# Alternating the halves of the accumulation bank between pairs of heads in a chunked RWKV-7 recurrence

## The chip, the cores and the metric

The kernel runs on one core of a Trainium2 chip. It is written with explicit instructions for the engines: TensorE (PE, matrix products, which write to PSUM banks of 128 partitions x 512 float32), VectorE (DVE), ScalarE (ACT), GpSimd (POOL) and SyncE, which issues transfers. The metric is the time of one execution on the device, in microseconds, as the median of several runs.

## The reference, cut to what matters

The program is one layer of a decoder trunk for 256 tokens of width 2048, all in float32: a mixer, an MLP and a gated embedding. Half of the mixer is an RWKV-7 recurrence with 16 heads of 64 channels:

```python
def step(S, inp):
    r_t, w_t, k_t, v_t, a_t, b_t = inp
    sa = jnp.einsum('bhij,bhj->bhi', S, a_t)
    S = S * w_t[:, :, None, :] + sa[..., None] * b_t[:, :, None, :] + v_t[..., None] * k_t[:, :, None, :]
    y = jnp.einsum('bhij,bhj->bhi', S, r_t)
    return S, y
...
mu = jnp.mean(y, axis=-1, keepdims=True)
var = jnp.mean(jnp.square(y - mu), axis=-1, keepdims=True)
y = (y - mu) * lax.rsqrt(var + GN_EPS) * gn_g.astype(f32).reshape(H, N) + gn_b.astype(f32).reshape(H, N)
```

Around it stand the other half of the mixer (moving averages over 2, 4, 8 and 16 tokens with a product), the products with `w_in`, `w_out`, the MLP (2048 to 8192 and back) and the gate.

## The kernel before, in words

**Chunks instead of steps.** The recurrence is not run token by token. The 256 tokens are cut into four chunks of 64, and the 16 heads into two groups of eight (`gi` 0 and 1), that is four pairs of heads each. Within a chunk everything is a product of small matrices. For each group, earlier stages make: `AR`, the decayed rows (for each pair and chunk, 64 columns for the state's reading `a` and 64 for the output's reading `r`, in the order i = 0, 1); `SC`, the masked scores of the chunk, whose upper left part has been replaced by the inverse of a triangular matrix; `UV`, with corrections `u` in partitions 0 to 63 and centred values `v` in 64 to 127; `BKt`, the decayed sources for the state's update.

**`rwkv_core(gi, st)`** runs the four chunks one after the other. A chunk `c` has one PSUM bank `b` (`rym`), whose lower 64 partitions collect the right-hand sides and whose upper 64 collect the outputs, 64 columns for each head:

1. `direct` (L695) adds the part of the right-hand sides that doesn't need the state; contraction over partitions 64 to 127. For chunk 0 it stands alone; for the later chunks it is issued one chunk ahead, head by head between the products of step 4. `bank(c)` (L691) first issues a product of one zero column with the start flag into the upper half, so that the outputs there accumulate from a clean state.
2. For c > 0 one product per pair (L707, 128x128) adds the state `cur` read through `AR[:, p, c]`: the 64 `a` columns go to the lower half of the bank, the 64 `r` columns to the upper.
3. ACT copies the lower half to SBUF as `R` (L713, 64x512).
4. The inverse is applied: `ub = SC[0:64, 0] x R` (L727), and ACT copies it to `UV[c][0:64]` (L731).
5. For c < 3 the state's update `sb` (L736) is computed; even heads go to partitions 0 to 63 and odd heads to 64 to 127 of another bank. ACT (c = 0, L745) or DVE (L747, after a decay in L718) puts it into the next state.
6. The outputs: `SC[:, 1] x UV[c]` for each head, added to the upper half of `b` (L749), and ACT copies it to `yss` (L754, 64x512).
7. For chunks 1 and 3, `group_norm` (L777 to L781) and, one chunk later, `group_out` (L787, L789).

A float32 product is two instructions in the trace, so the eight heads of a step are 16.

**What fills the waits.** PE's order is written out by hand (`manual_schedule`): the text of the program is PE's order. Between the steps stands `fill(us)`, which takes products of the queued large matrix products (`zv`, `zp`, `o0a`, `o1a`...; L164 to L166 and L173 to L175) for about the given microseconds by a fixed estimate per product, so their number between two steps is fixed. Each of them needs its weights split in two parts: ACT writes a rounded copy `wh` (L151, two instructions), DVE the remainder `wl` (L152), from three buffers. The order on the other engines comes from a planner with priorities; splits have 20000, the evacuations of `R` and `ub` 30000. `group_norm` has 25000.

**Beside it.** While the first group's core runs, DVE also works on `inverse(1, st1)` for the second group, 31 steps of two instructions (L621, L625), then four transposes (L630, L634), which ACT writes back into `SC` (L638). `rwkv_merge` (L649) uses it. While the second group's core runs there is no such work.

**Tiles.** Work tiles come from one pool by tag; a tag with one buffer is handed on when the last reader of the tile before is done. Tag `tA` holds the decay `P` of the second group until `rwkv_r(1)` has read it (L546), then nothing until the pooling after the first core. Tag `tE` is the work tile `tmp` of `inverse(1)` until ACT has read it out.

Of the kernel before, what the change touches and what calls it, by code (L numbers as in the profile page):

```python
# [9 lines left out]
F32 = mybir.dt.float32  # L10
F32R = mybir.dt.float32r
AF = mybir.ActivationFunctionType
# [28 lines left out]
def trunk(  # L41
# [19 lines left out]
    nc = tc.nc  # L61

    const = ctx.enter_context(tc.tile_pool(name="const", bufs=1))
# [9 lines left out]
    def rw_bank(name):  # L73
        return psr.tile([128, 512], F32, tag="rw", name=name)
# [33 lines left out]
    nc.gpsimd.memset(rmask.rearrange("p (c t) -> p c t", t=64)[:, :, 0:1], 0.0)  # L108
    for i in range(2):
        nc.vector.memset(sbd[i], 0.0)  # L110
    zero64 = const.tile([128, 64], F32, name="zero64")
    nc.vector.memset(zero64, 0.0)
    edge = const.tile([128, 4, 16], F32, name="edge")
    nc.vector.memset(edge, 1.0)
    for g, win in enumerate(WINDOWS):
# [118 lines left out]
    def fill(us):  # L234

        while us > 0 and queue:
            us -= advance()
# [44 lines left out]
    def e4(tag):  # L282
        return rp.tile([128, 4, T], F32, tag=tag, name=f"{tag}_t")
# [55 lines left out]
    for kg, (tg, n) in enumerate((("tE", 1), ("tF", 2), ("zk", 3), ("zr", 3), ("zv", 3), ("BK", 2), ("BKt", 2))):  # L339
# [13 lines left out]
        if kg == 4:  # L353
            for tt in range(2):
                for i, q in enumerate((2, 3)):
                    nc.tensor.matmul(
                        sbank[:, tt : tt + 1], sums[q][:, 0, tt * 128 : (tt + 1) * 128], ones[:, 0:1],
                        start=i == 0 and tt == 0, stop=i == 1, skip_group_check=True,
# [83 lines left out]
    def yb(gi, i):  # L442
        if gi == 0:
            return ybuf[:, i * 1024 : (i + 1) * 1024].rearrange("p (a t) -> p a t", a=4)
        return e4(("tF", "tC")[i])
# [235 lines left out]
    def rwkv_core(gi, st):  # L681
        AR, pc, SC, BKt, UV = st["AR"], st["pc"], st["SC"], st["BKt"], st["UV"]

        YT = yb(gi, 1)
        Rs = rp.tile([64, 2, 8, 64], F32, tag="q2", name=f"R{gi}")
        yss = rp.tile([128, 2, 8, 64], F32, tag="q3", name=f"ys{gi}")

        def bank(c):

            b = rw_bank("rym")  # L690
            nc.tensor.matmul(b[64:128, 0:1], zero64[64:128], zero64[64:128, 0:1], start=True, stop=False, skip_group_check=True)  # L691
            return b

        def direct(b, c, h):
            nc.tensor.matmul(  # L695
                b[0:64, h * 64 : h * 64 + 64], SC[64:128, 0, c, h, :], UV[c][64:128, h, :],
                start=h == 0, stop=c == 0, skip_group_check=True,
            )

        b = bank(0)  # L700
        for h in range(8):
            direct(b, 0, h)
        for c in range(4):
            cur, nxt = sbd[c % 2], sbd[(c + 1) % 2]
            if c > 0:
                for p in range(4):
                    nc.tensor.matmul(  # L707
                        b[:, p * 128 : p * 128 + 128], AR[:, p, c].rearrange("j i t -> j (i t)"), cur[:, p, :],
                        start=False, stop=False, skip_group_check=True,
                    )  # L710
            R = Rs[:, c % 2]
            with tc.high_priority(30000):
                nc.scalar.activation(flat3(R), b[0:64, :], AF.Copy)  # L713
            if 0 < c < 3:
                for e in range(2):
                    r = slice(e * 64, e * 64 + 64)
                    with tc.high_priority(30000):
                        nc.vector.tensor_tensor(  # L718
                            nxt[r, :, r], cur[r, :, r], pc[r, :, c : c + 1].to_broadcast([64, 4, 64]), op=ALU.mult
                        )  # L720
            fill(1.1)
            ub = rw_bank("um")
            if c < 3:
                sb = rw_bank("sm")
                b_next = bank(c + 1)
            for h in range(8):
                nc.tensor.matmul(ub[0:64, h * 64 : h * 64 + 64], SC[0:64, 0, c, h, :], R[:, h, :], start=True, stop=True)  # L727
                if c < 3:
                    direct(b_next, c + 1, h)
            with tc.high_priority(30000):  # L730
                nc.scalar.activation(flat3(UV[c])[0:64], ub[0:64, :], AF.Copy)  # L731
            fill(1.1)
            if c < 3:
                for h in range(8):
                    e, p = h % 2, h // 2
                    nc.tensor.matmul(  # L736
                        sb[e * 64 : e * 64 + 64, p * 64 : p * 64 + 64], BKt[:, c, p, e * 64 : e * 64 + 64], UV[c][:, h, :],
                        start=True, stop=True,
                    )
                add = sb[:, 0:256].rearrange("j (p i) -> j p i", i=64)  # L740
                for e in range(2):
                    r = slice(e * 64, e * 64 + 64)
                    with tc.high_priority(30000):
                        if c == 0:
                            nc.scalar.activation(nxt[r, :, r], add[r], AF.Copy)  # L745
                        else:
                            nc.vector.tensor_tensor(nxt[r, :, r], nxt[r, :, r], add[r], op=ALU.add)  # L747
            for h in range(8):
                nc.tensor.matmul(  # L749
                    b[64:128, h * 64 : h * 64 + 64], SC[:, 1, c, h, :], UV[c][:, h, :],  # L750
                    start=False, stop=True, skip_group_check=True,
                )
            ys = yss[:, c // 2]
            nc.scalar.activation(flat3(ys)[(c % 2) * 64 : (c % 2) * 64 + 64], b[64:128, :], AF.Copy)  # L754
            b = b_next
            if c == 1:
                norm0 = group_norm(gi, 0, yss[:, 0])
            if c == 2:
                group_out(gi, 0, norm0, YT)
            if c < 3:  # L760
                fill(1.6)
        return YT, st["rk"], yss
# [7 lines left out]
    def flat3(t_):  # L770
        return t_.rearrange("s h i -> s (h i)")

    def group_norm(gi, tt, ysb):
        with tc.high_priority(25000):
            vs = rp.tile([128, 8], F32, tag="gv", bufs=2, name=f"gv{gi}{tt}")
            sq = rp.tile([128, 8, 64], F32, tag="sq", name=f"sqy{gi}{tt}")
            nc.scalar.activation(sq, ysb, AF.Square)  # L777
            nc.vector.tensor_reduce(vs, sq, axis=AX.X, op=ALU.add)
            nc.scalar.activation(vs, vs, AF.Sqrt, bias=eps_g, scale=1.0 / 64.0)
            nc.vector.reciprocal(vs, vs)  # L780
            nc.vector.tensor_tensor(ysb, ysb, vs.unsqueeze(2).to_broadcast([128, 8, 64]), op=ALU.mult)  # L781
        return ysb

    def group_out(gi, tt, ysb, YT):
        b = rw_bank("yt")
        for p in range(4):
            nc.tensor.transpose(b[:, p * 128 : (p + 1) * 128], flat3(ysb)[:, p * 128 : (p + 1) * 128], ident)  # L787
        for p in range(4):
            nc.scalar.activation(  # L789
                YT[:, p, tt * 128 : (tt + 1) * 128], b[:, p * 128 : (p + 1) * 128], AF.Identity,  # L790
                scale=col("gn_g", 4 * gi + p), bias=col("gn_b", 4 * gi + p),
            )
# [122 lines left out]
    beside += [inverse(1, st1), 0.95, 0.0]  # L915
    fill(1.5)
    core0 = rwkv_core(0, st0)
    mg0 = a8(0, "mg0", F32R)
    rwkv_out(0, *rwkv_norm1(0, *core0), mg0)
# [30 lines left out]
    ]  # L950
    fill(1.5)
    core1 = rwkv_core(1, st1)
    finish(p_zp1)
    pws1 = pool_weights(1)
# [400 lines left out]
```

## Time and profile before

The median of three runs is 1205.03 us, from 1204.11 to 1207.36. The page shows one profiled execution, with a span of 1198.9 us; no time of its own beside that span is given for it.

| what | value |
|---|---|
| median of runs | 1205.03 us |
| span of the profiled execution | 1198.9 us |
| PE, DVE, ACT, POOL busy in it | 1179.6, 868.1, 687.7, 15.4 us |
| first core (chunks of group 0) | about 194 to 228 us |
| second core (group 1) | about 272 to 306 us |
| L749, one instruction | 0.22 us, x128 |

A row of the order of time has the start in us from the beginning of the span, the duration, the engine, the line, the operation, what is written from what, the shape and the count. Consecutive instructions of one kind are merged: the duration then runs from the first start to the last end. In brackets stands the idle time of the engine before the row and what ended it. Matrix products overlap, so a duration of 0.22 us does not mean that the next starts 0.22 us later; the distance of the starts has to be read.

### The profile page before, as it was taken

Reading aid. Unit: us, or ns where it says so; the run is one execution under the profiler, and the core shown is the slowest. Engines: PE = TensorE matmul, PEld = TensorE weight load, DVE = VectorE, ACT = ScalarE, POOL = GpSimd, SP = SyncE. Lnnn points to the kernel's source line nnn. Section 1 sums busy time; section 2 is a strip of 40 time slices with the busy share of each in tenths; the row PEclk is TensorE's granted clock in tenths of the full one; section 3 lists DMA queues with packets and bytes.
Section 4 is the critical chain, followed back from the end, with each engine's and each line's share of the span. In section 5 each row is a group of like instructions: output and inputs, shape, how many; then the busy total and the mean of one; then the engine's idle time right before and its main releaser. Section 6 shows DMA issues by size and latency. Waiting matters only on the chain.

```text
span 1198.9 us, 18442 instructions
## 1 busy us (share of the span) xinstructions
PE 1179.6 (98%) x7076; PEld 1013.6 (85%) x7076; DVE 868.1 (72%) x1150; ACT 687.7 (57%) x1260; POOL 15.4 (1%) x65
## 2 busy tenths in 40 slices
PE   8999999999999999999999999999999999999996
PEld 6999988988888888888888788888888888778886
DVE  8687987854556667666888878666667888887552
ACT  6857565665545556555555555555555655668544
POOL 4000000000000000000000000000000000000000
PEclk9999999999999999999999999999999999999999
DMA  7463542354355565666665666665565655776631
GB/s 250 151 202 110 173 155 95 121 186 142 116 177 169 185 185 191 192 193 189 194 203 197 197 197 203 195 187 189 192 193 178 211 198 191 290 234 219 194 121 71
DMA packets 60328, 216.88 MB, mean 181 GB/s; under 512 B 6736, under 2 KB 7120, under 8 KB 59856
## 3 DMA queue, kind: packets, MB, share of 16 engines
q1 hardware_dynamic: 59952, 215.19, 55.1%
q8 instruction: 55, 0.90, 0.3%
q10 hardware_dynamic: 288, 0.52, 0.1%
q14 instruction: 33, 0.27, 0.1%
HBM read 213.59 MB, written 2.10 MB: 180 GB/s over the span
## 4 chain that ended last, share of the span: by engine, by line
PE 81%; DMA 6%; DVE 6%; ACT 4%; issue 2%; SPq 0%; ACTq 0%; DVEq 0%
PE u_w L986 20%; PE u_w L990 10%; DMA raw_d<-in_w_ffn_down_dram 5%; PE d_b L1101 4%; PE d_b L1100 4%; PE d_b L1102 4%; PE gt_b L173 2%; PE gt_b L175 2%; PE gt_b L174 2%; PE zv_b L164 1%; PE zp_b L173 1%; PE wag_b L333 1%; PE zv_b L165 1%; PE zv_b L166 1%; PE zp_b L175 1%
## 5 line engine op out<-in xcount | busy, mean ns | idle before, releaser
L986 PE MATMUL u_w<-h,wh_u 128*128 128x512 f32 x1024 | 355.4, 393 | 0.0
L990 PE MATMUL u_w<-h,wl_u 128*128 128x256 f32 x1024 | 285.5, 279 | 0.0
L151 ACT ACTIVATE wh_u<-raw_u 128x512 fp32r<-128x512 f32 x256 | 147.6, 624 | 162.9 <-PE u_w L986 82.0
L152 DVE TENSOR_TENSOR wl_u<-raw_u,wh_u 128x1024 fp32r<-128x1024 f32 x128 | 156.6, 1224 | 112.1 <-ACT wh_u L151 112.1
L986 PEld LDWEIGHTS u_w<-h,wh_u 128*128 128x128 f32 x1024 | 191.8, 187 | 43.2
L990 PEld LDWEIGHTS u_w<-h,wl_u 128*128 128x128 f32 x1024 | 193.1, 189 | 0.1
L152 DVE TENSOR_TENSOR wl_gt<-raw_gt,wh_gt 128x1024 fp32r<-128x1024 f32 x24 | 29.4, 1225 | 23.9 <-ACT wh_gt L151 23.9
L151 ACT ACTIVATE wh_gt<-raw_gt 128x512 fp32r<-128x512 f32 x48 | 27.8, 631 | 23.0 <-PE gt_b L175 20.4
L1140 DVE TENSOR_TENSOR td<-raw_d 128x512 f32<-128x512 f32 x22 | 15.2, 692 | 33.9 <-DMA raw_d<-in_w_ffn_down_dram 33.9
L164 PE MATMUL zv_b<-hTh,wh_zv 128*128 128x256 f32 x128 | 37.7, 294 | 0.0
L173 PE MATMUL gt_b<-wh_gt,h 128*128 128x512 f32 x96 | 37.5, 390 | 0.0
L164 PE MATMUL zr_b<-hTh,wh_zr 128*128 128x256 f32 x128 | 37.5, 293 | 0.0
L175 PE MATMUL gt_b<-wh_gt,h 128*128 128x512 f32 x96 | 37.4, 389 | 0.0
L174 PE MATMUL gt_b<-wl_gt,h 128*128 128x512 f32 x96 | 37.4, 389 | 0.0
L166 PE MATMUL zr_b<-hTh,wl_zr 128*128 128x256 f32 x128 | 37.2, 290 | 0.1
L164 PE MATMUL zk_b<-hTh,wh_zk 128*128 128x256 f32 x128 | 37.0, 289 | 0.0
L165 PE MATMUL zr_b<-hTl,wh_zr 128*128 128x256 f32 x128 | 36.9, 288 | 0.0
L165 PE MATMUL zk_b<-hTl,wh_zk 128*128 128x256 f32 x128 | 36.3, 284 | 0.5 <-DVE hTl L157 0.5
L166 PE MATMUL zk_b<-hTh,wl_zk 128*128 128x256 f32 x128 | 36.3, 284 | 0.2 <-DVE wl_zk L152 0.2
L166 PE MATMUL zv_b<-hTh,wl_zv 128*128 128x256 f32 x128 | 36.2, 283 | 0.0
L165 PE MATMUL zv_b<-hTl,wh_zv 128*128 128x256 f32 x128 | 36.2, 283 | 0.0
L156 ACT ACTIVATE wad<-raw_d 128x512 fp32r<-128x512 f32 x22 | 13.9, 632 | 36.6 <-DMA raw_d<-in_w_ffn_down_dram 34.5
(804 smaller groups left out, 3081.4 us busy)
## 6 DMA issues: line engine op xcount, KB each, us to landing
raw_u<-in_w_ffn_up_dram SPq DMA_DIRECT2D x128, 512.0 KB, 3.5
raw_d<-in_w_ffn_down_dram SPq DMA_DIRECT2D x128, 512.0 KB, 4.2
raw_gt<-in_w_ple_gate_dram SPq DMA_DIRECT2D x24, 512.0 KB, 3.5
raw_zk<-in_w_in_dram SPq DMA_DIRECT2D x16, 512.0 KB, 3.3
raw_zr<-in_w_in_dram SPq DMA_DIRECT2D x16, 512.0 KB, 3.3
raw_zv<-in_w_in_dram SPq DMA_DIRECT2D x16, 512.0 KB, 3.3
raw_zp<-in_w_in_dram SPq DMA_DIRECT2D x16, 512.0 KB, 3.2
raw_o<-in_w_out_dram SPq DMA_DIRECT2D x16, 512.0 KB, 3.5
```

The costliest lines, as they stand in the source:

```text
L151: nc.scalar.activation(wh[:, a * 512 : (a + 1) * 512], raw[:, a * 512 : (a + 1) * 512], AF.Copy)
L152: nc.vector.tensor_tensor(wl, raw, wh.bitcast(F32), op=ALU.subtract)
L164: nc.tensor.matmul(o, w_h, ah, start=first and ct % 2 == 0, stop=False, skip_group_check=True)
L165: nc.tensor.matmul(o, w_h, al, start=False, stop=False, skip_group_check=True)
L166: nc.tensor.matmul(o, w_l, ah, start=False, stop=last, skip_group_check=True)
L173: nc.tensor.matmul(o, a_h, wh[:, 0:n], start=first, stop=False)
L174: nc.tensor.matmul(o, a_h, wl[:, 0:n], start=False, stop=False)
L175: nc.tensor.matmul(o, a_l, wh[:, 0:n], start=False, stop=last)
L986: nc.tensor.matmul(bank[:, ct, :].rearrange("p (s t) -> p s t", s=2), wh[:, c], hl, start=k == 0, stop=False, skip_group_check=True,)
L990: nc.tensor.matmul(bank[:, ct, 0:T], wl[:, c], hl[:, 0, :], start=False, stop=k == 15, skip_group_check=True)
L1100: nc.tensor.matmul(banks[n], ah, wh, start=first, stop=False)
L1101: nc.tensor.matmul(banks[n], ah, wl, start=False, stop=False)
```

## The change

For the pairs 1 and 3 of a group (heads 2, 3, 6 and 7) the two halves of the bank are swapped: their right-hand sides are collected in partitions 64 to 127 and their outputs in 0 to 63. The other heads stay as they were. The heads are issued in the order 0, 2, 1, 3, 4, 6, 5, 7, so that neighbours write to different halves. The product with the state needs `AR` with its two blocks of 64 columns exchanged for these pairs; two copies on POOL make this tile `ARs` at the start of the core, for chunks 1 to 3. The start flag is now set by the first head of each half (0 and 2), and the zero product and its tile are gone. An evacuation is no longer one block of 64 partitions: `two_halves` copies it in two instructions, each of 64 partitions and two runs of 128 columns. The products `ub` and the state's update are as before, except for the order of the heads in `ub`.

```diff
-    zero64 = const.tile([128, 64], F32, name="zero64")
-    nc.vector.memset(zero64, 0.0)
...
-        def bank(c):
-
-            b = rw_bank("rym")
-            nc.tensor.matmul(b[64:128, 0:1], zero64[64:128], zero64[64:128, 0:1], start=True, stop=False, skip_group_check=True)
-            return b
+        ARs = e4("tE" if gi else "tA").rearrange("j a t -> j (a t)")[:, 0:768]
+        ARs = ARs.rearrange("j (q c i t) -> j q c i t", q=2, c=3, i=2)
+        for i in range(2):
+            nc.gpsimd.tensor_copy(ARs[:, :, :, 1 - i], AR[:, 1::2, 1:4, i])
+
+        heads = (0, 2, 1, 3, 4, 6, 5, 7)
+
+        def half(h, y):
+
+            r = 64 if (h // 2 % 2 == 1) != y else 0
+            return slice(r, r + 64)
+
+        def two_halves(dst, b, y):
+
+            d = flat3(dst).rearrange("s (q r x) -> s q r x", q=2, r=2)
+            v = b.rearrange("s (q r x) -> s q r x", q=2, r=2)
+            for r in range(2):
+                nc.scalar.activation(d[:, :, r], v[half(2 * r, y), :, r], AF.Copy)
...
-                b[0:64, h * 64 : h * 64 + 64], SC[64:128, 0, c, h, :], UV[c][64:128, h, :],
-                start=h == 0, stop=c == 0, skip_group_check=True,
+                b[half(h, False), h * 64 : h * 64 + 64], SC[64:128, 0, c, h, :], UV[c][64:128, h, :],
+                start=h in (0, 2), stop=c == 0, skip_group_check=True,
             )
...
                 for p in range(4):
+                    ar = ARs[:, p // 2, c - 1] if p % 2 else AR[:, p, c]
                     nc.tensor.matmul(
-                        b[:, p * 128 : p * 128 + 128], AR[:, p, c].rearrange("j i t -> j (i t)"), cur[:, p, :],
+                        b[:, p * 128 : p * 128 + 128], ar.rearrange("j i t -> j (i t)"), cur[:, p, :],
...
-                nc.scalar.activation(flat3(R), b[0:64, :], AF.Copy)
+                two_halves(R, b, False)
...
-                b_next = bank(c + 1)
-            for h in range(8):
+                b_next = rw_bank("rym")
+            for h in heads:
...
-            for h in range(8):
+            for h in heads:
                 nc.tensor.matmul(
-                    b[64:128, h * 64 : h * 64 + 64], SC[:, 1, c, h, :], UV[c][:, h, :],
+                    b[half(h, True), h * 64 : h * 64 + 64], SC[:, 1, c, h, :], UV[c][:, h, :],
                     start=False, stop=True, skip_group_check=True,
                 )
-            ys = yss[:, c // 2]
-            nc.scalar.activation(flat3(ys)[(c % 2) * 64 : (c % 2) * 64 + 64], b[64:128, :], AF.Copy)
+            two_halves(yss[(c % 2) * 64 : (c % 2) * 64 + 64, c // 2], b, True)
```

More of the change, by code (lines that the diff above doesn't have):

```diff
@@ L686, in rwkv_core @@
         yss = rp.tile([128, 2, 8, 64], F32, tag="q3", name=f"ys{gi}")
-        def bank(c):
-            b = rw_bank("rym")
-            nc.tensor.matmul(b[64:128, 0:1], zero64[64:128], zero64[64:128, 0:1], start=True, stop=False, skip_group_check=True)
-            return b
+        ARs = e4("tE" if gi else "tA").rearrange("j a t -> j (a t)")[:, 0:768]
[11 more added lines that the diff above has]
+                nc.scalar.activation(d[:, :, r], v[half(2 * r, y), :, r], AF.Copy)
         def direct(b, c, h):
             nc.tensor.matmul(
-                b[0:64, h * 64 : h * 64 + 64], SC[64:128, 0, c, h, :], UV[c][64:128, h, :],
-                start=h == 0, stop=c == 0, skip_group_check=True,
-            )
-        b = bank(0)
-        for h in range(8):
+                b[half(h, False), h * 64 : h * 64 + 64], SC[64:128, 0, c, h, :], UV[c][64:128, h, :],
+                start=h in (0, 2), stop=c == 0, skip_group_check=True,
+            )
+        b = rw_bank("rym")
+        for h in heads:
             direct(b, 0, h)
@@ L747, in rwkv_core @@
                             nc.vector.tensor_tensor(nxt[r, :, r], nxt[r, :, r], add[r], op=ALU.add)
-            for h in range(8):
+            for h in heads:
                 nc.tensor.matmul(
-                    b[64:128, h * 64 : h * 64 + 64], SC[:, 1, c, h, :], UV[c][:, h, :],
+                    b[half(h, True), h * 64 : h * 64 + 64], SC[:, 1, c, h, :], UV[c][:, h, :],
                     start=False, stop=True, skip_group_check=True,
                 )
-            ys = yss[:, c // 2]
-            nc.scalar.activation(flat3(ys)[(c % 2) * 64 : (c % 2) * 64 + 64], b[64:128, :], AF.Copy)
+            two_halves(yss[(c % 2) * 64 : (c % 2) * 64 + 64, c // 2], b, True)
             b = b_next
```

## The prediction

> **What bounds the kernel now.** I read the page first (spans, engines, chain), then the busy time by stage around the two recurrences, then the matmuls of the bank tile, and last the order of time there, engine by engine.
>
> ```profile
> span 1198.9 us, 18442 instructions
> PE 1179.6 (98%) x7076; PEld 1013.6 (85%) x7076; DVE 868.1 (72%) x1150; ACT 687.7 (57%) x1260; POOL 15.4 (1%) x65
> PE 81%; DMA 6%; DVE 6%; ACT 4%; issue 2%; SPq 0%; ACTq 0%; DVEq 0%
> ...
> 194.00:230.00 36.00, 36.00 (x433) 33.35 (x432) 33.85 (x82) 20.06 (x38) 0.00 (x0) 1.00 0.29 99
> 272.00:307.00 35.00, 35.00 (x360) 28.39 (x359) 16.04 (x23) 20.92 (x39) 0.00 (x0) 1.00 0.42 136
> ```
>
> The matmul engine is 98% busy and carries 81% of the chain. The last two rows are the stages that change: the first recurrence (194 to 230 us) and the second (272 to 307). Columns after the window: its length, then busy time of PE, weight loads, DVE, ACT and POOL, the granted clock (1.00) and DMA. PE is full in both. The second resource differs: DVE is busy 33.85 of 36 us in the first stage, because the inversion for the second head group runs there, but only 16.04 of 35 in the second. A saving on PE is therefore worth different amounts in the two stages, and the busy column can't show it; the starts of the instructions can.
>
> ```profile
> 200.21 0.68 PE L736 MATMUL sm<-UV,BKt 128*64 128x64 f32 x16
> 200.73 1.10 PE L749 MATMUL rym<-UV,SC 128*64 128x64 f32 x16
> 201.75 0.39 PE L164 MATMUL zv_b<-hTh,wh_zv 128*128 128x256 f32 x1
> ...
> 194.96 1.03 PE L695 MATMUL rym<-UV,SC 64*64 64x64 f32 x15
> ...
> 197.63 0.22 PE L727 MATMUL um<-R,SC 64*64 64x64 f32 x1
> 197.64 0.22 PE L695 MATMUL rym<-UV,SC 64*64 64x64 f32 x1
> 197.69 0.22 PE L727 MATMUL um<-R,SC 64*64 64x64 f32 x1
> ```
>
> L736 and L749 have the same shape, contraction 128 to 64 outputs, 16 instructions each (two per head). L736 already alternates between the lower and upper 64 output partitions from head to head; L749 writes all heads to the upper ones. One instruction lasts 0.22 us, so the starts are (0.68 - 0.22) / 15 = 0.031 us apart in L736 and (1.10 - 0.22) / 15 = 0.059 in L749. That is the effect which the change wants, measured in this kernel.
>
> **The change part by part.**
>
> *Output products (L749), 8 blocks.* With alternating halves I take L736's pace: 16 x (0.059 - 0.031) = 0.45 us saved per block, 1.8 us per recurrence. The bounds are 0, if accumulating into a bank behaves differently from L736, and the whole distance of the two starts, 201.75 - 200.73 less 200.73 - 200.21 = 0.50.
>
> *First direct products (L695 alone), 2 blocks.* 15 instructions in 1.03 us: (1.03 - 0.22) / 14 = 0.058 apart. In the new order they alternate too: 0.45 us each, same bounds.
>
> *Direct products beside the corrections (L727, L695), 6 blocks.* L727 and L695 already start 0.01 us apart, and the next L727 0.06 after the last. L727 stays in the lower half, 16 steps of 0.058; it sets the pace, whichever half L695 uses. Gain 0. If the two stopped overlapping, each block would cost 16 x 0.058 = 0.93 more; nothing in the rows suggests it.
>
> *Zero products (L691) and their tile.* They start together with the first real one (206.08, next fence), so I take 0; at most 0.08 us for each of 8 blocks. The decayed-state products (L707) only read another tile for odd pairs: 0.
>
> So PE has 10 x 0.45 = 4.5 us less to issue, 2.25 per recurrence.
>
> *Evacuations in two pieces.* The nearest row for a piece of 64x256 from PSUM is L745.
>
> ```profile
> 201.14 0.77 ACT L745 ACTIVATE sbd<-sm 64x256 f32<-64x256 f32 x2
> 204.75 0.59 ACT L713 ACTIVATE R<-rym 64x512 f32<-64x512 f32 x1 [2.23 <-PE rym L707]
> 206.08 0.21 PE L691 MATMUL rym<-zero 64*64 64x1 f32 x1
> 206.08 0.27 PE L727 MATMUL um<-R,SC 64*64 64x64 f32 x1
> 207.26 0.59 ACT L731 ACTIVATE UV<-um 64x512 f32<-64x512 f32 x1 [0.88 <-PE um L727]
> 208.79 0.69 PE L736 MATMUL sm<-UV,BKt 128*64 128x64 f32 x16
> 213.85 0.30 ACT L779 ACTIVATE gv<-gv,eps_g 128x8 f32<-128x8 f32 x1 [1.11 <-DVE gv L778]
> 214.17 0.59 ACT L713 ACTIVATE R<-rym 64x512 f32<-64x512 f32 x1
> 214.82 0.27 PE L727 MATMUL um<-R,SC 64*64 64x64 f32 x1
> ```
>
> Two pieces take 0.77 instead of 0.59: +0.18 us, 16 times, 2.9 us of ACT, which has 14 us and more free in each stage. For the right-hand sides the product L727 waits: the one at 204.75 ends at 205.34 and is wanted at 206.08, so 0.74 us of other matmuls hide it and 0.56 remain. In one place nothing hides it: at 214.17 ACT comes late out of a normalisation that waits for DVE, R ends at 214.76 and L727 starts at 214.82. There PE starts 0.18 us later, at a time that DVE sets. The pieces for the outputs have no early reader; behind them on ACT stand weight splits.
>
> *What DVE allows in the first recurrence.*
>
> ```profile
> 227.99 1.14 DVE L630 STREAM_TRANSPOSE T1G<-X 32x512 f32<-32x512 f32 x1
> 228.97 1.20 DVE L152 TENSOR_TENSOR wl_zv<-raw_zv,wh_zv 128x1024 fp32r<-128x1024 f32 x1
> 230.41 0.28 PE L166 MATMUL zv_b<-hTh,wl_zv 128*128 128x256 f32 x1
> ...
> 235.69 2.13 ACT L638 ACTIVATE SC<-tmp 32x1024 f32<-32x1024 f32 x2 [1.41 <-DVE tmp L634]
> 260.05 2.14 PE gm L649 x64
> ```
>
> DVE runs its list nearly back to back here (33.85 of 36 us, and no idle time is noted before its rows). The split of 228.97 ends at 230.17 and PE uses it at 230.41: 0.24 us of slack. Nothing that DVE does before it gets shorter, so PE can be at most 0.24 us early at that point, however much it saved (and the stop at 214.82 has already taken back what c=0 and c=1 gave). Of 2.25 us I book 0.24. The lower bound of the gain is 0, the upper 2.25 if DVE's order of instructions comes out differently.
>
> *The second recurrence.* DVE and ACT have room, and their splits wait for PE, so most of the saving moves them along. Two splits are tight.
>
> ```profile
> 281.86 1.22 DVE L152 TENSOR_TENSOR wl_o0a<-raw_o0a,wh_o0a 128x1024 fp32r<-128x1024 f32 x1 [2.20 <-ACT wh_o0a L151]
> 283.18 0.39 PE L174 MATMUL o0a_b<-wl_o0a,mg 128*128 128x512 f32 x1
> 304.43 1.15 ACT L151 ACTIVATE wh_o1a<-raw_o1a 128x512 fp32r<-128x512 f32 x2 [1.00 <-PE o1a_b L175]
> 305.61 1.23 DVE L152 TENSOR_TENSOR wl_o1a<-raw_o1a,wh_o1a 128x1024 fp32r<-128x1024 f32 x1 [3.70 <-ACT wh_o1a L151]
> 307.13 0.40 PE L174 MATMUL o1a_b<-wl_o1a,mg 128*128 128x512 f32 x1
> ```
>
> The first has 0.10 us of slack. By then PE has saved 0.90, but the output pieces (+0.18 on ACT) stand ahead of this split, which comes only 0.72 earlier: PE gains 0.82. The second is released by PE before the last L749 block, so it moves 0.82 + 2 x 0.45 = 1.72, and its slack of 0.29 takes up only part of the last 0.45: 2.01 us gained in all.
>
> *The swapped copies.* Two POOL copies of 128x384 per group. The nearest rows give 0.28 us for 128 elements and 0.17 for 2, so 0.0009 us per element and some 0.5 us per copy. In the second group the tile is free when ACT has read the inversion out (L638, 237.8), long before the stage that begins at 272. In the first group it is free when DVE has read P at 167.41.
>
> ```profile
> 5.01 0.28 POOL L99 COPY jsum<-cmask 128x128 f32<-128x128 f32 x1
> 5.24 0.17 POOL L103 COPY jhead<-cmask 128x2 f32<-128x2 f32 x1
> 166.20 1.21 DVE L546 TENSOR_TENSOR AR<-zr_t,tA_t 128x1024 f32<-128x1024 f32 x1
> 167.34 1.26 DVE L554 SCALAR_TENSOR_TENSOR tF_t<-zr_t,par_sb,tE_t 128x256 f32<-128x256 f32 x3
> 169.72 1.20 DVE L152 TENSOR_TENSOR wl_zp<-raw_zp,wh_zp 128x1024 fp32r<-128x1024 f32 x1
> 170.93 0.39 PE L174 MATMUL zp_b<-wl_zp,hTh 128*128 128x512 f32 x1
> 12.25 1.60 POOL L126 TENSOR_SCALAR_AFFINE_SELECT wband<-wband 128x144 f32<-128x144 f32 x2
> 13.31 0.39 DVE L128 TENSOR_TENSOR wband<-wband,ident 128x128 f32<-128x128 f32 x1
> 14.51 0.28 DVE L128 TENSOR_TENSOR wband<-wband,ident 128x128 f32<-128x128 f32 x1
> ```
>
> Their first use is in the second chunk, after the block that begins at 200.73, so the copies themselves are hidden. But they run while DVE works towards the split of 169.72, which ends 0.01 us before PE wants it. At 13.31 DVE's subtraction took 0.39 us beside POOL's select and 0.28 at another time: 0.11 for an overlap, 0.2 us for two copies. Bounds: 0, and both copies whole, 1.0.
>
> The Trainium skill, "SBUF — State Buffer", section "Who interferes with whom", says that a VectorE instruction with two SBUF inputs contends with a GpSimd one that reads SBUF, and that the later one is blocked for the whole instruction. By that rule DVE could lose both copies, and the saving in the sum below would be 1.25 us in place of 2.05. The overlap at 13.31 cost far less than a whole POOL instruction, so the trace does not bear out the full price.
>
> *Sum.* -0.24 - 2.01 + 0.2 = -2.05 us. The profiled span becomes 1198.9 - 2.05 = 1196.9. The median stands 6.1 us above that span, work around it which does not change: 1205.03 - 2.05 = **1203.0 us**, 0.17% faster.
>
> **The rivals.**
>
> *A. DVE's order gives way.* The order on DVE and ACT is planned anew; if the splits move ahead of the inversion's steps, the first recurrence keeps its 2.25. Then -4.5 + 0.2: 1200.7. For it: the inversion's result is read out by 237.8 us and not wanted until 260.05, so its steps have room. Against: the plan's inputs hardly change.
>
> *B. POOL blocks DVE fully.* The copies wait between DVE's steps at 167.4 and each costs it 0.5: +1.0 in place of 0.2 at 170.93, and everything after it is later: 1203.8. For it the 0.01 us of slack; against it the row at 13.31.
>
> *C. Slower: evacuations get behind splits.* With one more piece to place, ACT's order may put a pair of splits (1.15 us, row of 304.43) ahead of an evacuation that PE waits for. The right-hand sides have 0.56 us of cover left, so each such place costs 0.59; the corrections' evacuations, with 0.94 of cover (207.85 to 208.79), 0.21. At all eight places of each kind: 8 x 0.59 + 8 x 0.21 = 6.4, and 1203.0 + 6.4 = 1209.4. It decides the sign from 2.05 us, four places. Against: such pairs now mostly run in the gaps (2.23 us idle before 204.75).
>
> *D. No pairing.* If alternation brings nothing in L749, only the added costs stay: +0.2 to +0.5, about 1205.4. L736 speaks against it.
>
> **How the numbers follow.** Forecast 0.38, A 0.28, B 0.10, C 0.19, D 0.05. Under 0.3% (3.6 us) this kernel's runs can't tell from no change. Faster by more: A and 0.03 of the forecast's spread, 0.31. Slower by more: C and 0.02 for an order worse still elsewhere, 0.21. Within: 0.48. The range reaches past A, to 1199.9, and up to 1207.6 with part of C; the forecast's own is 1201.8 to 1204.0.
>
> **What would show it.** L749's 16 instructions in about 0.68 us instead of 1.10, and the same for the first L695 blocks; L727 and L695 together unchanged. Two ACT pieces of 0.38 each. In the first recurrence gaps between PE's starts at the splits' first uses and at the L727 near 215; in the second nearly none. POOL's copies near 167.5 and 238. I am wrong if DVE's splits come at other places in its list, if PE waits for R in several blocks, or if PE's starts stay 0.059 apart.

## The result and the profile after

The changed kernel takes 1200.63 us in the median (1195.48 to 1204.58), the kernel before 1204.4 us on the same chip. The ratio is 0.9963, with a 95% interval of 0.9951 to 0.9974: 4.5 us faster by the ratio, and 3.8 by the two medians. The forecast was 1203.0.

The page of the changed kernel (span, busy engines, shares of the chain):

```profile
span 1199.6 us, 18428 instructions
PE 1179.5 (98%) x7060; PEld 1010.6 (84%) x7060; DVE 868.5 (72%) x1149; ACT 689.8 (58%) x1276; POOL 18.1 (2%) x69
PE 81%; DVE 8%; DMA 4%; ACT 4%; issue 2%; SPq 0%; ACTq 0%; DVEq 0%
```

The page doesn't show the gain. PE is 98% busy and carries 81% of the chain as before; DVE's share of the chain is 8% where it was 6%. This span is even longer than that of before (1198.9), because the two are single executions and the time of one program scatters by 9 us from run to run. An execution's own time is its span and some 1.7 us (after: 1201.35 us in all), so the profiled execution of before took about 1200.6 us, a quick one. What can be compared to hundredths is a stretch of PE's order that the program fixes. In both kernels I take the start of a recurrence's first direct product (with the zero product that starts with it before the change) and of the first transpose (`yt`) at its end. Order of time, kernel before:

```profile
194.85 0.27 PE L695 MATMUL rym<-UV,SC 64*64 64x64 f32 x1
236.63 0.27 PE L787 MATMUL yt<-ident,ys 128*128 128x128 f32 x1
272.30 0.21 PE L691 MATMUL rym<-zero 64*64 64x1 f32 x1
314.40 0.27 PE L787 MATMUL yt<-ident,ys 128*128 128x128 f32 x1
```

And the kernel after (start, duration, engine, line, tiles, shape, count):

```profile
196.19 0.68 PE L706 MATMUL rym<-UV,SC 64*64 64x64 f32 x16
196.80 0.50 PE L171 MATMUL zp_b<-wh_zp,hTh 128*128 128x512 f32 x1
...
198.50 0.22 PE L739 MATMUL um<-R,SC 64*64 64x64 f32 x1
198.56 0.22 PE L739 MATMUL um<-R,SC 64*64 64x64 f32 x1
...
201.07 0.69 PE L748 MATMUL sm<-UV,BKt 128*64 128x64 f32 x16
201.59 0.64 PE L761 MATMUL rym<-UV,SC 128*64 128x64 f32 x16
202.16 0.39 PE L162 MATMUL zv_b<-hTh,wh_zv 128*128 128x256 f32 x1
...
236.21 0.38 PE L798 MATMUL yt<-ident,ys 128*128 128x128 f32 x2
271.88 0.68 PE L706 MATMUL rym<-UV,SC 64*64 64x64 f32 x16
311.61 0.38 PE L798 MATMUL yt<-ident,ys 128*128 128x128 f32 x2
```

The first recurrence shrank from 236.63 - 194.85 = 41.78 us to 40.02, the second from 42.10 to 39.73; the work between them is 35.67 us in both. Together that is 1.76 + 2.37 = 4.13 us of the 4.5. The source of it is in the same rows. The output products (L761, 16 of them) last 0.64 us where the block took 1.10, so they now start (0.64 - 0.22) / 15 = 0.028 us apart instead of 0.059. From the block's start to the next block it is 202.16 - 201.59 = 0.57 us, against 1.02 before. The first direct products take 196.80 - 196.19 = 0.61, before about 1.08. The corrections beside direct products (L739, L706) still start one L739 every 0.06.

The second recurrence keeps all five blocks' saving (5 x 0.46 = 2.3). The first loses some of it, and these rows show where. DVE and PE, chunk 2:

```profile
211.46 0.86 DVE L759 TENSOR_TENSOR sbd<-sbd,sm 64x256 f32<-64x256 f32 x2
...
212.03 0.28 PE L164 MATMUL zv_b<-hTh,wl_zv 128*128 128x256 f32 x1
212.38 0.49 PE L719 MATMUL rym<-sbd,AR 128*128 128x128 f32 x2
```

DVE's state update (L759) ends at 211.46 + 0.86 = 212.32, and the product that reads it (L719) starts at 212.38, although the filling product before it began at 212.03 and the usual distance is 0.12. The 15 filling products and the wait take 2.12 us instead of 1.90, the four state products 0.91 instead of 0.81; the same happens in chunk 3 with 0.06 and 0.10. What the update itself stood behind is in DVE's rows. PE and DVE after the change, then DVE and PE before it:

```profile
209.18 0.69 PE L748 MATMUL sm<-UV,BKt 128*64 128x64 f32 x16
209.77 0.42 DVE L619 TENSOR_TENSOR tmp<-X,AT 64x255 f32<-64x255 f32 x1
...
211.12 0.42 DVE L623 TENSOR_TENSOR X<-X,tmp 64x256 f32<-64x256 f32 x1
```

```profile
211.05 0.86 DVE L747 TENSOR_TENSOR sbd<-sbd,sm 64x256 f32<-64x256 f32 x2
212.24 1.06 PE L707 MATMUL rym<-sbd,AR 128*128 128x128 f32 x8
```

The products that the update adds (L748) have ended at 209.87, but DVE runs four instructions of the inversion's steps without a pause, from 209.77 on, before it comes to the update at 211.46. Before the change the update was late as well, but it ended at 211.91, 0.33 us before L707. The shorter blocks on PE have used that up. Later, ACT and PE:

```profile
213.58 0.78 ACT L703 ACTIVATE R<-rym 64x256 f32<-64x256 f32 x2 [0.56 <-PE rym L719]
215.85 0.30 ACT L790 ACTIVATE gv<-gv,eps_g 128x8 f32<-128x8 f32 x1 [1.50 <-DVE gv L789]
216.06 1.14 ACT L149 ACTIVATE wh_zv<-raw_zv 128x512 fp32r<-128x512 f32 x2
217.22 0.59 ACT L743 ACTIVATE UV<-um 64x512 f32<-64x512 f32 x1
...
217.87 0.69 PE L748 MATMUL sm<-UV,BKt 128*64 128x64 f32 x16 [0.19 <-ACT UV L743]
```

The right-hand sides (L703) now stand ahead of the normalisation's square root (L790) on ACT; before they stood behind it (gv at 213.85, R at 214.17), which stopped PE near 215. That stop, 0.16 us, is gone. In its place the corrections' evacuation (L743) stands behind the square root, which waited 1.50 us for DVE (its sum `gv`, at 215.15 on DVE, now stands behind the split of 214.02; before, at 213.14, it stood ahead of that of 213.74), and behind two weight splits, and the state update on PE starts late: 1.88 us of filling in place of 1.62. The balance of the first recurrence: 2.3 saved, 0.32 + 0.16 lost to DVE's state update, 0.26 to the late evacuation, 0.16 won at the old stop: 1.72, against 1.76 measured.

The copies on POOL, and DVE beside the first two:

```profile
168.57 1.94 POOL L689 COPY tA_t<-AR 128x384 f32<-128x384 f32 x2 [12.73 <-DVE AR L544]
239.04 0.96 POOL L689 COPY tE_t<-AR 128x384 f32<-128x384 f32 x2 [68.52 <-ACT SC L636]
...
168.44 1.26 DVE L552 SCALAR_TENSOR_TENSOR tF_t<-zr_t,par_sb,tE_t 128x256 f32<-128x256 f32 x3
```

The two copies of the second group take 0.96 us and those of the first 1.94. The first copy alone bears the difference: it takes 1.49 us, while DVE's L552 runs three times, and the second takes 0.50. DVE's three instructions take 1.26 us as before the change. So POOL lost the time and DVE did not.

### The profile page after: what moved, and what is told of

Read it like the earlier page. It is cut to its first block, busy times and chain, and to the rows that moved or that the text cites. A ratio compares the mean times of both kernels' runs of the same rounds, so it can differ in the third digit from the quotient of the medians.

```text
span 1199.6 us, 18428 instructions
## 1 busy us (share of the span) xinstructions
PE 1179.5 (98%) x7060; PEld 1010.6 (84%) x7060; DVE 868.5 (72%) x1149; ACT 689.8 (58%) x1276; POOL 18.1 (2%) x69
## 4 chain that ended last, share of the span: by engine, by line
PE 81%; DVE 8%; DMA 4%; ACT 4%; issue 2%; SPq 0%; ACTq 0%; DVEq 0%
PE u_w L997 20%; PE u_w L1001 10%; PE d_b L1112 5%; PE d_b L1113 5%; PE d_b L1111 5%; DMA raw_d<-in_w_ffn_down_dram 3%; PE gt_b L171 2%; PE gt_b L173 2%; PE gt_b L172 2%; PE wag_b L331 1%; PE zp_b L171 1%; PE o_b L171 1%; PE o_b L172 1%; PE o_b L173 1%; PE d_w L1112 1%
```

## The experiments

Two readings had to be told apart. One: the gain is PE's pairing alone, and waits on DVE and ACT take part of it back in the first recurrence. The other: part of the gain comes from the new order on ACT and DVE (the evacuation in two pieces, the new plan), not from the pairing. The lengths of the fixed stretches (us, from start to start as above; rounded from finer starts, so that two rows can give 0.01 more or less), and the ratios to the kernel before with their 95% intervals:

| kernel | first | between | second | sum | ratio |
|---|---|---|---|---|---|
| before | 41.78 | 35.67 | 42.10 | 119.55 | |
| after | 40.01 | 35.67 | 39.73 | 115.42 | 0.9963 (0.9951 to 0.9974) |
| after, again | 40.03 | 35.67 | 39.73 | 115.44 | 0.996 (0.9944 to 0.9975) |
| second group alone | 41.75 | 35.67 | 39.73 | 117.16 | 0.9983 (0.9965 to 1.0001) |
| first group alone | 40.02 | 35.67 | 42.10 | 117.79 | 1.001 (0.9997 to 1.0023) |
| first group alone, again | 40.03 | 35.67 | 42.10 | 117.81 | 0.9991 (0.9971 to 1.0011) |
| heads in order | 40.07 | 35.67 | 40.07 | 115.82 | 0.9987 (0.997 to 1.0004) |
| corrections too | 38.58 | 35.67 | 37.93 | 112.19 | 0.993 (0.9908 to 0.9951) |
| before, no steps | 45.35 | 35.67 | 42.16 | 123.19 | 1.001 (0.999 to 1.003) |
| after, no steps | 43.53 | 35.67 | 39.73 | 118.93 | 0.9985 (0.9964 to 1.0006) |
| pieces alone | 41.63 | 35.67 | 42.10 | 119.41 | 0.9989 (0.9971 to 1.0007) |
| merge too | 38.89 | 33.66 | 38.17 | 110.72 | 0.9887 (0.9864 to 0.991) |
| half steps | 43.17 | 35.67 | 39.73 | 118.57 | 0.9998 (0.9979 to 1.0017) |

### One group alone

```diff
-        heads = (0, 2, 1, 3, 4, 6, 5, 7)
+        sw = gi == 1
+        heads = (0, 2, 1, 3, 4, 6, 5, 7) if sw else tuple(range(8))
...
-            r = 64 if (h // 2 % 2 == 1) != y else 0
+            r = 64 if (sw and h // 2 % 2 == 1) != y else 0
```

This is the second group alone; the other kernel has `gi == 0`. The group without the change has the zero product, the order of heads and the single evacuation of before.

> Only the second group of heads alternates between the halves; the first group is as before. Theory (each recurrence keeps what DVE lets it keep): the second recurrence is 2.3 us shorter, from its first direct product to the transposes after its end, the first one as long as before (77.4 us from one recurrence's first direct product to the next one's); time about 2.3 us below the kernel before. Rival (the gain lies in the first recurrence or elsewhere, by another order of the planned engines): less than 1 us, or a first stage of another length.

> Only the first group alternates. Theory: PE saves 2.3 us and DVE, whose order puts the splits earlier than before, takes back about 0.5, so 1.8 us below the kernel before. Rival, my forecast's ceiling (the split near 230 us holds PE): 0.24 us below. The second recurrence as long as before (42.1 us from its first direct product to the transposes after its end).

Order of time, second group alone, then first group alone:

```profile
271.54 0.68 PE L719 MATMUL rym<-UV,SC 64*64 64x64 f32 x16
311.27 0.60 PE L811 MATMUL yt<-ident,ys 128*128 128x128 f32 x4
```

```profile
195.02 0.68 PE L719 MATMUL rym<-UV,SC 64*64 64x64 f32 x16
235.04 0.60 PE L811 MATMUL yt<-ident,ys 128*128 128x128 f32 x4
```

The second group alone has 311.27 - 271.54 = 39.73 us, the full saving of 2.37, and its first recurrence is that of before. The first group alone has 235.04 - 195.02 = 40.02, the 1.76 of the whole change, and its second recurrence is that of before. The two parts add up to the whole: 2.37 + 1.76 = 4.13. The time of the second group alone agrees (0.17% is 2.0 us), though its interval just reaches 1. For the first group alone the times don't settle it: the same program gave 1.001 and 0.9991, and 1.76 us would be 0.9985, outside the first interval and inside the second. So the saving of the first group is seen in the stage and not in the time; where it went in those executions I did not find. Both profiled executions had the longer pace in half of the up-projection (last section), but so had those of the changed kernel, which did gain.

> The first group alone, again: its recurrence was 1.76 us shorter in the trace, yet the time was not below that of the kernel before. In the traces so far the two halves of the first MLP product run at one of two steady paces (22.19 or 22.61 us for 128 products, 3.3 us over a half), now the one and now the other. If the pace is drawn anew in every execution, the first group alone comes out 1 to 2.5 us below before this time. If it belongs to the program, this profile shows the fast pace in the first half and the slow one in the second, as the first time, and the time is again as before.

### Heads in the order 0 to 7

```diff
-        heads = (0, 2, 1, 3, 4, 6, 5, 7)
+        heads = tuple(range(8))
```

> The changed kernel with its heads issued in the old order 0 to 7, so that two heads in a row use the same half. Theory (two products overlap only where neighbours in the order use different halves): in a block of 16 instructions 3 steps instead of 7 are hidden; from the first start to the last 0.72 us, against 0.88 before and 0.46 changed; 1.5 us below the kernel before in all, or less where DVE holds PE. Rival (it is enough that the heads lie in two halves): blocks as in the changed kernel and 4.5 us below.

Order of time, one pair of blocks in the second recurrence:

```profile
275.79 0.69 PE L748 MATMUL sm<-UV,BKt 128*64 128x64 f32 x16
276.31 0.68 PE L761 MATMUL rym<-UV,SC 128*64 128x64 f32 x16
```

I had expected a saving of only 1.5 us, since two heads in a row then use the same half. Nearly all of it stays: the output block lasts 0.68 us against 0.64, and the stages together are 115.82 us, only 0.40 longer than after (ten blocks, 0.04 us each). So strict alternation from head to head is not needed; the starts come two by two, 0.004 and then 0.054 us apart. The ratio, 0.9987, shows less than a saving of 3.73 us would (0.9969, just below its interval); the last section has a possible part of that.

### The corrections paired as well

```diff
-                nc.tensor.matmul(ub[0:64, h * 64 : h * 64 + 64], SC[0:64, 0, c, h, :], R[:, h, :], start=True, stop=True)
+                nc.tensor.matmul(ub[half(h, False), h * 64 : h * 64 + 64], SC[0:64, 0, c, h, :], R[:, h, :], start=True, stop=True)
...
-                nc.scalar.activation(flat3(UV[c])[0:64], ub[0:64, :], AF.Copy)
+                two_halves(UV[c][0:64], ub, False)
```

> The changed kernel, and the corrections (the product with the inverse) go to alternating halves as well, evacuated in two pieces. Theory (the corrections set the pace of their blocks because all are in the lower half): the blocks shorten from 1.07 to 0.6 us, 8 x 0.46 = 3.7 us less for PE; the second recurrence keeps 1.8 of it, the first between 0 and 1.8: 6.2 to 8.1 us below the kernel before. Rival (products of the two row halves and the two column halves can't all overlap): blocks stay at 1.07, time as the changed kernel, 4.4 us below, or worse by the added pieces.

Order of time, chunk 0:

```profile
199.26 0.27 PE L739 MATMUL um<-R,SC 64*64 64x64 f32 x1
199.27 0.27 PE L706 MATMUL rym<-UV,SC 64*64 64x64 f32 x1
199.28 0.27 PE L739 MATMUL um<-R,SC 64*64 64x64 f32 x1
199.28 0.27 PE L706 MATMUL rym<-UV,SC 64*64 64x64 f32 x1
...
199.89 0.50 PE L171 MATMUL zp_b<-wh_zp,hTh 128*128 128x512 f32 x1
```

Four products of 64x64 start within 0.02 us: two with contraction over the lower partitions (corrections) and two over the upper (direct), each kind into both halves of outputs. The block takes 199.89 - 199.26 = 0.63 us instead of 1.07. In the second recurrence all of it arrives: 4 x 0.45 = 1.80 = 39.73 - 37.93. In the first 1.43 arrives; PE's state update in chunk 2 again waits for the corrections' evacuation on ACT. The time follows, 0.7% below before. This confirms the pairing as the cause, with a block that the change itself left alone.

### The inversion's steps left out

```diff
         for k in range(31):
+            if gi:
+                yield
+                continue
```

> The kernel before, with the 31 steps of the second group's inversion left out, so that DVE has little beside the splits in the first recurrence. It gives the reference for the next run. Theory (DVE's splits hold PE in the first recurrence only): here 41.6 us or a little less from the first direct product to the transposes after the end, since the one stop near 215 us goes with the load on DVE. Rival: 41.8 as before, DVE's load has no part in it.

> The changed kernel, with the same 31 steps left out. Theory: without that load the first recurrence keeps what the second does, 2.3 to 2.4 us less than the kernel before without the steps: about 39.3 us in place of the changed kernel's 40.0. Rival (the loss of 0.6 us in the first recurrence comes from the pieces on ACT, not from DVE): still 1.8 us less, 39.9.

ACT in the kernel before without the steps:

```profile
201.23 2.14 ACT L641 ACTIVATE SC<-tmp 32x1024 f32<-32x1024 f32 x2 [1.40 <-DVE tmp L637]
203.39 0.59 ACT L734 ACTIVATE UV<-um 64x512 f32<-64x512 f32 x1
```

Leaving the steps out moved the inversion's read-out into chunk 0, where its 2.14 us on ACT stand ahead of the corrections' evacuation. So chunk 0 became longer in both kernels (3.82 and 4.36 us of filling before the state update, against 1.60), and the difference of the two first recurrences, 1.82 us, can't be read as the saving without DVE's load. The later chunks can: from chunk 2 on both run without any of the waits above (1.90 us of filling before chunk 2's state products, 0.81 for these, 1.63 before its state update) and differ by the paired blocks alone. The inversion's place in the lists of DVE and ACT is therefore what the lost 0.74 us hangs on. That the work itself on DVE is the cause is not shown by this run. For the 0.48 us at the state update, DVE's rows of the first section show it: steps stand between the products and the update.

### Half steps

```diff
+            m = (m + 1) // 2 if gi else m
...
-                AT[:, k, n:32].unsqueeze(1).to_broadcast([64, n, m]), op=ALU.mult,
+                AT[:, k, n : n + m].unsqueeze(1).to_broadcast([64, n, m]), op=ALU.mult,
```

> The changed kernel, with each of the 31 inversion steps for the second group done on half of its columns only, so that DVE's steps are about 0.25 us long where they were 0.42, and end earlier. Theory (the 0.6 us that the first recurrence loses are waits for DVE's update of the state and its normalisation, which stand behind the steps in DVE's list): 39.3 to 39.7 us in place of 40.0. Rival (the loss is ACT's, whose list has 16 more pieces): 40.0.

ACT:

```profile
225.85 1.05 ACT L637 ACTIVATE SC<-tmp 32x1024 f32<-32x1024 f32 x1 [4.47 <-DVE tmp L633]
226.93 0.59 ACT L744 ACTIVATE UV<-um 64x512 f32<-64x512 f32 x1
```

DVE:

```profile
209.68 0.86 DVE L760 TENSOR_TENSOR sbd<-sbd,sm 64x256 f32<-64x256 f32 x2
```

With half the columns in each step the wait for the state update did not go; it grew (2.43 us of filling before chunk 2's state products, after the change 2.12). In chunk 3 the read-out again stands ahead of the corrections' evacuation, and 4.57 us pass there in place of 1.63. So the theory that shorter steps would end the waits is not borne out. DVE's list says why. The products that the update adds end at 207.77, and the update starts at 209.68: six step instructions of the halved length stand between, where there were four of the full one. Counted from the inversion's first step, 42 step instructions stand ahead of this update. In the changed kernel it is 32, in the kernel before and with the pieces alone 34, with the corrections paired as well 30. So the plan moves with the program, but in each kernel with all its steps it leaves some between the products and the update. An order with the update ahead of them was not run; what it would save stays open.

### The evacuation in two pieces alone

```diff
-                nc.scalar.activation(flat3(R), b[0:64, :], AF.Copy)
+                two_pieces(R, b[0:64])
...
-            nc.scalar.activation(flat3(ys)[(c % 2) * 64 : (c % 2) * 64 + 64], b[64:128, :], AF.Copy)
+            two_pieces(ys[(c % 2) * 64 : (c % 2) * 64 + 64], b[64:128])
```

This is the kernel before; both pieces come from the same half.

> The kernel before with its evacuations in two pieces each and nothing else. Theory (the pieces cost ACT 0.18 us each time and PE nothing but one stop of 0.18 near 215 us, and do not bring the order of DVE that helped): first recurrence 41.8 to 42.0 us, second 42.1; time as before. Rival (it is the pieces that made the planner put the splits earlier): first recurrence 41.6 or less.

ACT:

```profile
214.59 0.65 ACT L699 ACTIVATE R<-rym 64x256 f32<-64x256 f32 x2 [0.23 <-PE rym L714]
216.26 0.30 ACT L786 ACTIVATE gv<-gv,eps_g 128x8 f32<-128x8 f32 x1 [1.03 <-DVE gv L785]
```

The pieces alone put the right-hand sides ahead of the square root and remove the stop near 215: 41.63 us instead of 41.78. That is all that they give, 0.15 us. They leave DVE's order as it was. The order of DVE that comes with the alternation in the first group is therefore not tested by this run. But PE's blocks are just as short in the second recurrence, where no steps run on DVE.

### The merge products too, and the change once more

On top of the paired corrections, the 32x32 products that merge the inverse's quarters (L647, L654) alternate between two groups of 32 output partitions:

```diff
-                nc.tensor.matmul(b[32:64, u * 32 : u * 32 + 32], SCu[0:32, uu, 32:64], T1G[0:32, uu, :], start=True, stop=True)
+                r = 32 + 32 * (u % 2)
+                nc.tensor.matmul(b[r : r + 32, u * 32 : u * 32 + 32], SCu[0:32, uu, 32:64], T1G[0:32, uu, :], start=True, stop=True)
...
+            for e in range(2):
+                nc.scalar.activation(
+                    T1G[32:64, hf * 16 + e : hf * 16 + 16 : 2],
+                    b[32 + 32 * e : 64 + 32 * e, :].rearrange("t (u e j) -> t u e j", e=2, j=32)[:, :, e], AF.Copy,
+                )
```

> The kernel of e4 (corrections in alternating halves), and the 32x32 products of the merge alternate too, between two groups of 32 output partitions, with two ACT pieces for each evacuation. A block of 64 instructions takes 2.14 us now, 0.032 us from start to start. Theory (pairs to different output partitions start together, at the pace of one): 1.1 us a block, four blocks, up to 4 us less than e4, less what the longer read-out (0.18 us for each of 8 evacuations) shows on PE. Rival (0.032 us is near what an instruction takes to start, whatever its place): blocks of about 2 us and no gain over e4.

> The changed kernel once more. Its two recurrences took 40.0 and 39.7 us against 41.8 and 42.1; if they are fixed by the program they are the same to 0.1 us, and the time is 4.1 us below the kernel before. The step of the two MLP halves: if its pace belongs to the program, 22.2 us for 128 products in the first and 22.6 in the second, as before; if it is drawn in each execution it may differ.

Order of time, with the paired merge, and then the kernel after:

```profile
254.91 1.20 PE L648 MATMUL gm<-T1G,SC 32*32 32x32 f32 x64
256.04 0.50 PE L171 MATMUL zp_b<-wh_zp,hTh 128*128 128x512 f32 x1
```

```profile
259.56 2.21 PE L647 MATMUL gm<-T1G,SC 32*32 32x32 f32 x64
261.69 0.50 PE L171 MATMUL zp_b<-wh_zp,hTh 128*128 128x512 f32 x1
```

A block of 64 merge products takes 1.13 us in place of 2.13, and the stretch between the recurrences 33.66 in place of 35.67. Each recurrence gives back 0.2 to 0.3 us of what the paired corrections had. This version has 1192.05 us against 1205.16 of the kernel before: 13 us and 1.1% faster, the best of all here. Its stretches account for 119.55 - 110.72 = 8.8 us, and the first group's merge, which lies ahead of them, for 1.7 more; the remaining 2.6 I have not located. The change itself, run again, gave 0.996 and the same stages to 0.02 us.

## Why the prediction was right and wrong

The time, 1200.63, lies in the range (1199.9 to 1207.6), but near its lower end: the gain was 4.5 us and not 2.05, and the time is outside the forecast's own 1201.8 to 1204.0. It is rival A's size (1200.7). That the number is in the range is owed to the range's reach, not to the forecast's account of DVE, which was wrong. By the steps:

- **Output products and first direct products: right.** Forecast 0.45 us for each block, measured 0.46; the corrections beside direct products 1.07 as before, forecast unchanged. Rival D falls with it.
- **Zero products and swapped tile reads: right.** The state products take 0.81 us with the swapped tile where they don't wait.
- **Pieces: right in size.** The pair at 213.58 takes 0.78 us against the 0.77 taken from L745. The stop near 215 was forecast 0.18 us later; it went, because the plan put R ahead of the square root.
- **"What DVE allows in the first recurrence": wrong, and this is the step that failed.** I took the split of 228.97 to serve the product of 230.41, 0.24 us later, and booked 0.24 of 2.25. Names in the rows come without buffer numbers, so that was a product of the same name which used an earlier split. Counting settles it: the stage has 16 splits of `zv`, 8 of each half, and 24 products to each; the split of 228.97 is the last, and its 24 products are the last of `zv`. Order of time, kernel before:

```profile
233.05 0.28 PE L164 MATMUL zv_b<-hTh,wh_zv 128*128 128x256 f32 x1
233.29 0.28 PE L166 MATMUL zv_b<-hTh,wl_zv 128*128 128x256 f32 x1
```

They begin at 233.05, and the remainder (`wl`) that DVE made by 230.17 is first used at 233.29: a slack of 3.1 us, not 0.24. The other splits there had more. So 1.76 us of the 2.25 came through. What took the rest was not the splits but the state update on DVE and one evacuation on ACT, which the prediction didn't name as late next. The update had 0.33 us in hand (211.91 to 212.24).
- **Rival A: half of its way.** DVE's order did give way. In the changed kernel's list 20 step instructions stand ahead of the `zv` split of 203.22, where 22 stood ahead of the same split at 202.76, and 32 ahead of the state update, where there were 34. Two of them are 0.9 us (one starts every 0.45 there), so by estimate the update would have come some 0.9 us later without the move. The new order then let part of the saving through, at the state update. A looked for it at the splits, which had not been in the way.
- **The second recurrence: same error, smaller.** The two splits called tight did not hold PE; 2.37 us arrived in place of 2.01. After the change the second of them starts on DVE at 303.29 and ends at 304.51, but the product in the place of the one of 307.13 already starts at 304.34: it reads an earlier split.
- **The swapped copies: wrong side.** +0.2 was booked for DVE; DVE lost nothing, and rival B falls. Its 0.01 us of slack was misread too: by the same count (16 splits of `zp`, four remainder products to each) the split of 169.72 is first used at 174.96. The row for two copies is 1.94 us beside L552, against 0.96 in the second group. The Trainium skill, "SBUF — State Buffer", section "Who interferes with whom", says that of two instructions that share the port pair one is blocked fully and the order of issue decides which. The trace agrees that one side bears all; here it was POOL, with 1.0 us in one copy, and nobody waited for it.
- **Rival C: once, not eight times.** The corrections' evacuation got behind two splits in one place, 0.26 us.
- **"6.1 us above that span, work around it": wrong.** The work around a span is 1.7 us; the rest was the scatter of executions. It did not enter the difference.

With the measured terms the sum would have been -1.76 - 2.37 = -4.13, and the time 1205.03 - 4.13 = 1200.9 us.

## What to carry to other kernels

In this kernel, products that fill half of the array or a quarter gained by being spread over halves of output partitions, and over halves of contraction where two kinds stand side by side. The order needed no strict alternation (0.04 us for each block), and the price was one more evacuation piece. When a split or a load looks tight in a trace, find out by counting which product really uses it before the saving behind it is written off. A gain of a few us in a kernel whose executions scatter by 9 is read from stretches of an order that the program fixes, and the time is needed in addition, for what such stretches don't cover.

## What the runs showed of the hardware

**Places of the array.** On average, products of 128x64 start 0.028 us apart in alternating halves and 0.059 in one; four products of 64x64 start together every 0.06 us; products of 32x32 start 1.13 / 64 = 0.018 us apart over two groups of output partitions, and 2.13 / 64 = 0.033 in one. The Trainium skill, "TensorE: Matmul & The Clock Gate", section "Wait — 56ns, not 53.3ns?", says that the distance from start to start never drops below about 25 ns, however small the product. Within one place, 0.033 us, no run here contradicts it. Over two places 0.018 us was measured, and there the measurement decides.

**Two paces in the MLP.** In the up-projection, which no kernel here changes, 128 products take 22.19 us in some stretches and 22.61 in others at full granted clock, 3.3 us over half of the phase. Groups of lines in the window from 740 to 905 us, kernel before, then after (busy time, mean ns):

```profile
L986 PE MATMUL u_w<-h,wh_u 128*128 128x512 f32 x477 | 165.4, 394 | 0.0
```

```profile
L997 PE MATMUL u_w<-h,wh_u 128*128 128x512 f32 x469 | 165.8, 399 | 0.0
```

In the profiled executions of before and of the second group alone the whole phase had the shorter pace, in those of after its second half the longer, in that of the heads in order the whole phase. Each of the two programs that were run twice showed the same pace both times. If an execution always keeps it, it hides up to 16 x 0.42 = 6.7 us of a saving elsewhere, and would explain why the heads in order gained less time than their stages; but the paired merge had the longer pace too and gained more than its stages. Against a pace that belongs to the program stand the executions with the shorter pace in both halves. There were three, and each was quick among its program's runs: before by 3.8 us against the median (1200.6 to 1204.4), the second group alone by 7.4 (1196.37 to 1203.76) and the half steps by 7.2 (1197.95 to 1205.17). That fits a pace which differs from one execution to the next. It doesn't settle it, for the heads in order, with the longer pace throughout, were 3.3 under their median. The cause is open.
